# A two-layer encoder trunk on one Trainium2 core: the first layer's output projection as seven quarter products, and all five queues in an order read from a table

## The chip, the core and the metric

The kernel runs on one core of one Trainium2 chip. The metric is the device time of one execution in microseconds (us). Three executions of the kernel before took 652.29, 652.94 and 653.63 us; their median is 652.94 us. The engines are named as the profile names them: PE (TensorE, matmuls), PEld (its weight loads), DVE (VectorE), ACT (ScalarE), POOL (GpSimd), SP (SyncE, which issues most loads and stores).

## The reference

512 tokens of width 1024 pass two layers. Layer 0 mixes tokens with neighbourhood attention on a grid 64 wide (16 heads of 64), layer 1 with multi-head latent attention (MLA, 16 heads, dense over the 512 tokens). Both have the same frame:

```python
for i in range(2):
    xn = rmsnorm(x, norm_g[i])
    y = mixer_na(xn, ...) if i == 0 else mixer_mla(xn, ...)   # (heads(xn) * silu(z)) @ w_out
    h = x + y
    gate = sigmoid(rmsnorm(h, ple_norm[i]) @ ple_w_gate[i])
    x = h + gate * (p[i] @ ple_w_proj[i])
return rmsnorm(x, final_norm)
```

The mixer's input projection also gives `z`, as wide as the heads' outputs together. `w_out` and `ple_w_gate[i]` are 1024x1024. The change bears on `(heads * silu(z)) @ w_out` of layer 0 and on the order in which everything is issued.

## The kernel before

**Products.** Every float32 product is made of three matmuls on halves: an operand is copied to a rounded `hi` (ACT), `lo` is the rest (a subtraction on POOL or DVE), and hi·hi, lo·hi and hi·lo are added up in one PSUM bank. A weight piece (128x1024, 512 KB) is loaded by SP into one of three buffers `wraw`, ACT makes `hi` of it, POOL makes `lo` (`load_w`, L89 to L106; ACT's line is L100, the subtraction L101). A full 1024x1024 product over 512 tokens is 8 banks of 24 matmuls of 128x512, 192 in all (`out_proj`, L622 to L636).

**Seven products.** The values of layer 0 (`values_seven`) and the two gate matrices (`gate_seven`, L775) are already computed by a scheme of Strassen's kind: both operands are cut into quarters, seven products of sums of quarters replace eight, and 168 matmuls do the work of 192. The weight sums are made ahead in device memory by DMAs that POOL issues, some of them accumulating (`sum_step`, L726 to L730, eight of 1 MB for a matrix). The sums for layer 0's gate are made in heads 0 to 7 of layer 0, those for layer 1's gate in heads 8 to 15 (`na_heads`: `l, step = divmod(j, 4)`, where `j` is a pair of heads).

**Heads of layer 0.** For a pair `j`, `attend` (L493) calls `na_head` twice. One head makes scores on PE (L558, L559, bank `ps_S`), takes maxima on DVE (L565), exponentials on ACT (L576), reciprocals on DVE (L578), the normalization on POOL (L582, four instructions a head), transposes on PE (L594, L596, bank `ps_T`), splits the turned weights into `ph` and `pl`, and multiplies with the values (L608, bank `ps_O`). `combine` adds the two halves (L220 on ACT, L221 on DVE) and `gated` (L223 to L229) multiplies by `z` on POOL and splits into `oh` and `ol`. The last three `z` (NLATE) come after the last pair.

**The seam.** After the heads, `out_proj` does its 192 matmuls. Each bank is added to the residual `r` by DVE (L635), eight additions of 128x512, and handed to `turn_h` (L1258), which scales it, transposes it and lets `keep_half` (L745) form the operands of `gate_seven` from it.

**MLA heads.** In layer 1 `mla_heads` (L942) walks 64 quarter heads: scores (L123, `ps_S`), maximum on DVE (L1052), exponential on ACT (L1054), reciprocal on DVE (L1055), normalization on POOL (L1056), four transposes (L155), and products with the values (L1071). Projections of later heads (L959) fill PE in between. Queries are partly moved by DMA (`qe<-rl`).

**Order.** The program is traced as Python runs, and a scheduler that simulates a timeline then orders each engine's instructions (`schedule_with_timeline_sim`, in `kernel`). Some forty places pin an instruction behind another with `tc.issue_after`, among them the class `InOrder` (L41) and the chains of matmuls in `out_proj` and `gate_seven`. What a queue holds runs strictly in that queue's order.

## Time and profile before

| | |
|---|---|
| runs shown | 652.29, 652.94, 653.63 us; median 652.94 |
| the profiled execution | 653.56 us; span 651.5 us, granted clock 0.995 |
| outside the span | 653.56 - 651.5 = 2.06 us |
| busy share of the span | PE 98%, PEld 83%, ACT 70%, DVE 66%, POOL 63% |
| moved by DMA | 107.41 MB, mean 165 GB/s |

The span runs from the first to the last instruction of the profiled execution, which is itself one of the runs. A busy time counts the records of an engine as a union in time; a matmul's record includes its way through the array, so that the distance between the starts of neighbouring matmuls (their pitch) is what one of them costs in a row. In a timeline a row groups like instructions that follow each other: start, length, engine, line, operation, output and inputs, count, and in brackets the idle time before it and what ended that. Windows give each engine's busy time in a stretch with its count, then the granted PE clock, the DMA share and the GB/s. POOL's records overlap: the next one starts before the last has ended, and here too the pitch is the cost.

### The profile page before, as it was taken

What the parts mean: (1) busy time and instruction counts of PE and PEld (TensorE: products, weight loads), DVE (VectorE), ACT (ScalarE), POOL (GpSimd) and SP (SyncE); (2) the same over time, 40 slices, a digit from 0 to 9 for tenths busy, and PEclk for the clock granted to TensorE, in tenths of its full rate; (3) what the DMA queues carried; (4) which work ended last, traced back from release to release, by engine and by line L of the source; (5) the groups of instructions that cost most, each with busy time, mean ns of one, the idle gap of its engine ahead of it and who ended that gap; (6) DMA issues with size and microseconds to landing.
All of it is one profiled execution on the core that took longest, in us unless ns stands there. A gap on an engine that the chain in (4) does not pass through costs nothing.

```text
span 651.5 us, 9980 instructions
## 1 busy us (share of the span) xinstructions
PE 640.2 (98%) x3299; PEld 541.9 (83%) x3299; DVE 427.7 (66%) x886; ACT 453.4 (70%) x903; POOL 408.4 (63%) x371
## 2 busy tenths in 40 slices
PE   9999999999999999999999999999999999999994
PEld 6888878888888888888999887888888888888884
DVE  6197987565665616569715514898988885474665
ACT  7575766887886733788644535897989897547855
POOL 0471006877978853797655516786969887437974
PEclk9999999999999999999999999999999999999997
DMA  9939725778958989446643245120112223683524
GB/s 326 355 124 306 217 66 179 263 205 217 229 209 217 239 178 342 147 154 188 224 140 102 78 109 156 32 75 24 49 50 66 65 84 112 229 292 126 193 65 162
DMA packets 46131, 107.41 MB, mean 165 GB/s; under 512 B 4736, under 2 KB 17792, under 8 KB 46080
## 3 DMA queue, kind: packets, MB, share of 16 engines
q1 hardware_dynamic: 34608, 87.12, 39.3%
q0 software_dynamic: 11040, 18.88, 13.6%
q10 hardware_dynamic: 432, 0.79, 0.3%
q8 instruction: 26, 0.43, 0.3%
q14 instruction: 25, 0.20, 0.1%
HBM read 95.23 MB, written 25.17 MB: 185 GB/s over the span
## 4 chain that ended last, share of the span: by engine, by line
PE 83%; POOL 1%; ACT 1%; DVE 0%; DMA 0%; issue 0%; POOLq 0%
PE ps_mm L123 27%; PE ps_S L123 10%; PE ps_mm L959 7%; PE ps_T L155 6%; PE ps_T L851 5%; PE ps_O L1071 5%; PE ps_mm L851 3%; PE ps_S L851 3%; PE ps_O L608 2%; PE ps_T L123 2%; PE ps_O L123 2%; PE ps_mm L909 2%; PE ps_T L301 2%; PE ps_T L596 2%; PE ps_S L909 1%; PE ps_S L559 1%
## 5 line engine op out<-in xcount | busy, mean ns | idle before, releaser
L101 POOL TENSOR_TENSOR wwlo<-wraw,wwhi 128x1024 fp32r<-128x1024 f32 (+5 forms) x68 | 122.3, 1810 | 93.5 <-ACT wwhi L100 41.9
L796 POOL TENSOR_TENSOR wlo<-wraw,whi 128x512 fp32r<-128x512 f32 x56 | 72.7, 1331 | 22.3 <-ACT whi L794 20.2
L1056 POOL TENSOR_TENSOR ex<-ex,rc 128x512 f32<-128x512 f32 x64 | 66.2, 1043 | 26.6 <-DVE rc L1055 22.5
L100 ACT ACTIVATE wwhi<-wraw 128x1024 fp32r<-128x1024 f32 (+5 forms) x71 | 55.1, 799 | 34.3 <-PE ps_mm L123 18.9
L1054 ACT ACTIVATE ex<-ps_S,mx 128x512 f32<-128x512 f32 x64 | 44.0, 687 | 12.6 <-DVE mx L1052 10.9
L1052 DVE TENSOR_REDUCE mx<-ps_S 128x1 f32<-128x512 f32 x64 | 43.7, 683 | 8.4 <-PE ps_S L123 7.7
L582 POOL TENSOR_TENSOR ex<-ex,rc 128x128 f32<-128x128 f32 (+1 forms) x64 | 37.5, 701 | 17.7 <-DVE rc L578 17.5
L112 DVE TENSOR_TENSOR pt_lo<-ps_T,pt_hi 128x512 fp32r<-128x512 f32 x64 | 43.1, 680 | 7.1 <-ACT pt_hi L110 6.7
L110 ACT ACTIVATE pt_hi<-ps_T 128x512 fp32r<-128x512 f32 x64 | 37.7, 594 | 3.4 <-PE ps_T L155 3.0
L155 PE MATMUL ps_T<-ident,ex 128*128 128x128 f32 x256 | 38.3, 272 | 0.0
L155 PEld LDWEIGHTS ps_T<-ident,ex 128*128 128x128 f32 x256 | 31.5, 140 | 7.5
L123 PE MATMUL ps_mm<-xh,wwhi 128*128 128x512 f32 x120 | 33.7, 404 | 0.0
L221 DVE TENSOR_TENSOR u<-ps_O,u 64x512 f32<-64x512 f32 x32 | 21.9, 685 | 17.7 <-ACT u L220 17.2
L576 ACT ACTIVATE ex<-ex,mx 128x128 f32<-128x128 f32 (+1 forms) x64 | 30.2, 473 | 4.2 <-DVE mx L565 4.1
L123 PE MATMUL ps_mm<-xl,wwhi 128*128 128x512 f32 x120 | 31.9, 395 | 0.0
L794 ACT ACTIVATE whi<-wraw 128x1024 fp32r<-128x1024 f32 x28 | 29.3, 1057 | 3.2 <-DMA wraw<-sum 2.4
L123 PE MATMUL ps_mm<-xh,wwlo 128*128 128x512 f32 x120 | 31.1, 394 | 0.0
L123 PE MATMUL ps_S<-ke,qe 96*128 96x512 f32 x96 | 28.9, 407 | 0.3 <-DMA qe<-rl 0.3
L123 PE MATMUL ps_S<-ko,qo 128*128 128x512 f32 x96 | 28.9, 409 | 0.0
L959 PE MATMUL ps_mm<-cT,wwhi 128*128 128x512 f32 x94 | 27.7, 393 | 0.0
L220 ACT ACTIVATE u<-ps_O 64x512 f32<-64x512 f32 x32 | 18.9, 591 | 12.0 <-PE ps_O L608 8.8
L225 POOL TENSOR_TENSOR u<-u,z 128x512 f32<-128x512 f32 x16 | 22.6, 1412 | 7.5 <-DVE u L221 7.5
(488 smaller groups left out, 1915.1 us busy)
## 6 DMA issues: line engine op xcount, KB each, us to landing
sum<-gate POOLq DMA_DIRECT2D x12, 1024.0 KB, 8.2
wraw<-na_qk SPq DMA_DIRECT2D x16, 512.0 KB, 4.9
wraw<-sum SPq DMA_DIRECT2D x16, 512.0 KB, 3.3
pe<-pe SPq DMA_DIRECT2D x31, 256.0 KB, 5.9
wraw<-gate SPq DMA_DIRECT2D x12, 512.0 KB, 3.3
wraw<-na_v SPq DMA_DIRECT2D x10, 512.0 KB, 3.4
sum<-sum POOLq DMA_DIRECT2D x4, 1024.0 KB, 11.1
wraw<-na_o SPq DMA_DIRECT2D x8, 512.0 KB, 4.8
```

What stands on the lines that cost most here:

```text
L100: nc.scalar.activation(hi[:, c], raw[:, c], AF.Copy)
L101: f = lambda e, c=c: e.tensor_tensor(out=lo[:, c], in0=raw[:, c], in1=hi[:, c].bitcast(F32), op=ALU.subtract)
L110: self.last_copy = self.act.activation(hi, src, AF.Copy, scale=scale)
L112: self.dve.tensor_tensor(out=lo, in0=src, in1=hi.bitcast(F32), op=ALU.subtract)
L123: last = self.last_mm = nc.tensor.matmul(out, l, r, start=i == 0, stop=i == n - 1)
L155: self.last_mm = self.nc.tensor.transpose(t[:, i * P:(i + 1) * P], b, self.ident)
L796: nc.gpsimd.tensor_tensor(out=lo[:, o], in0=raw[:, o], in1=hi[:, o].bitcast(F32), op=ALU.subtract)
L851: mm = nc.tensor.matmul(ps, l, r, start=j == 0 and p in banks, stop=j == 11 and p in (2, 3, 4), skip_group_check=True)
L959: self.last_mm = nc.tensor.matmul(PS[key], *terms[i], start=i == 0, stop=i == len(terms) - 1)
L1052: nc.vector.reduce_max(mx, sp, axis=AX.X, negate=True)
L1054: nc.scalar.activation(ex, sp, AF.Exp, bias=mx, accum_out=sm)
L1056: nc.gpsimd.tensor_tensor(out=ex, in0=ex, in1=rc.to_broadcast([P, S]), op=ALU.mult)
```

## The change

1. **Seven products for layer 0's output projection** (`MIXED = (0,)`, `out_seven`): 7 products x 2 token halves x 12 = 168 matmuls of 128x512 take the place of 192. Its weights come in 14 pieces instead of 8 (6 from `na_o`, 8 from sums); the products' banks are 1, 7 and 6, and the four others are added on in the same banks. The left operands need sums as well: `gated_seven` forms them per `oT` block in halves of 256 columns, `mixes` takes three differences of 128x256 on DVE for four blocks, `cast` splits them. The additions into the residual become 18 instead of 8 (`adds`), all on DVE, and `keep_mixed` keeps the residual's halves in mixed form. The gate of layer 0 takes its products in the order 1, 7, 6, 2, 5, 3, 4.
2. **Sums in other places**: the eight DMAs for `na_o` are issued in heads 0 to 7 of layer 0, those for layer 0's gate in heads 8 to 15, and those for layer 1's gate in MLA heads 1 to 8.
3. **Heads in parts**: `na_head` ends after the normalization; the transposes with their splits (`na_turn`) and the products with the values (`na_out`) are functions of their own. In the last pair both heads' scores come first, then the late `z`, then a string `BEFORE` gives the order of what is left; a string `INSIDE` gives that of `out_seven`.
4. **The order**: all `issue_after` pins go. `ORDER` holds a permutation of each engine's traced instructions, and `in_order` ties every instruction behind the one before it in that list. The scheduler has nothing left to choose on the five queues, in the whole program.

The diff, cut to its core (the table is one line of some 190):

```diff
+MIXED = (0,)
+BEFORE = """t00 t01 m0 W70w W71w g5 g6 h0 t10 t11 W20w h1 g7"""
+INSIDE = """
+W21vd P10 P11 m01 y01 a10 m02 y02 a11 W40vd P70 P71 W41v a70 m03 y03 a71 W60vd W61vd
...
-            with self.tc.issue_after(self.last.ins) if self.last is not None else nullcontext():
-                self.last = call(*args, **kw)
+            self.last = call(*args, **kw)
...
             for j in range(8):
-                l, step = divmod(j, 4)
-                if step == 0:
-                    self.quarters(l)
-                attend(j, lambda e: self.sum_step(l, 2 * step + e))
-            late = range(8 - NLATE, 8)
-            zs.update(self.z_phase(a["na_z"], xT, late, self.last_exp.ins))
-            for j in late:
-                self.gated(U[j], zs[j], oT, j)
+                key = (("out", 0), ("gate", 0))[j // 4]
+                if j == 5:
+                    self.W, self.oT = {}, oT
+                    for c in range(2):
+                        self.out_piece(None, 0, 1, c, str(c))
+                (attend if j < 7 else lambda j, also: last_pair(also))(j, lambda e: self.sum_step(key, 2 * (j % 4) + e))
...
+    def gated_seven(self, u, zs, oT, j):
+        z = zs[j]
+        self.pool.tensor_tensor(out=z, in0=u, in1=z, op=ALU.mult)
+        g, k = divmod(j, 4)
+        hi, lo = (oT[s][g][:, k, :] for s in range(2))
+        if g == 0:
+            self.pool.tensor_tensor(out=u[:, HI], in0=z[:, LO], in1=z[:, HI], op=ALU.subtract)
+            for x, c in ((z, LO), (u, HI)):
+                self.act.activation(hi[:, c], x[:, c], AF.Copy)
+                self.pool.tensor_tensor(out=lo[:, c], in0=x[:, c], in1=hi[:, c].bitcast(F32), op=ALU.subtract)
+            return
+        self.act.activation(hi, z, AF.Copy)
+        (self.pool if j == 4 else self.dve).tensor_tensor(out=lo, in0=z, in1=hi.bitcast(F32), op=ALU.subtract)
...
+        def product(p, i, mm):
+            m = [(x[s][:, k, o + i * P:o + (i + 1) * P], W[p][k // 2][r][:, k % 2 * S:(k % 2 + 1) * S])
+                 for c in range(2) for s, r in ((0, 0), (1, 0), (0, 1)) for k in (2 * c, 2 * c + 1)]
+            for j, (l, r) in enumerate(m):
+                self.last_out = nc.tensor.matmul(ps, l, r, start=j == 0 and p in banks,
+                                                 stop=j == 11 and p in (2, 4, 3), skip_group_check=True)
...
             nc.vector.reciprocal(rc, sm)
-            nc.gpsimd.tensor_tensor(out=ex, in0=ex, in1=rc.to_broadcast([P, S]), op=ALU.mult)
+            norm = nc.gpsimd.tensor_tensor(out=ex, in0=ex, in1=rc.to_broadcast([P, S]), op=ALU.mult)
+            step = h - 1
+            if qt == 1 and 0 <= step < 8:
+                self.sum_step(("gate", 1), step)
...
+ORDER = dict(
+    PE=(
+        "0-10 23 29-30 24-25 31-32 11-12 26 13 35 14-16 20-21 27 53 17-19 41 47 42-43 48-50 54 51 36 28 22 37-38 52 63 "
...
+def in_order(tc):
+    behind = mybir.DependencyInfo(mybir.DependencyClass.NoSync, mybir.DependencyReason.DATA)
+    for e, runs in ORDER.items():
+        mine = [i for i in traced if i.engine == getattr(mybir.EngineType, engines[e])]
...
+        for x, y in zip(order, order[1:]):
+            tc.add_manual_dep(y, x.name, behind, reason="in_order")
```

Three places show what the order does. First PE at the start of the output projection. Before, the first two banks (`ps_S_2697`, `ps_S_2737`) take their matmuls in runs of two, from the weight pieces `wwhi_2599` and `wwhi_2605` and the operands `oh0`, `ol0`:

```order
L596 MATMUL ps_T_2388<-ident_71,ex_2351 128x128 x4
L123 MATMUL ps_S_2697<-wwhi_2599,oh0_1000 128x512 x2
L123 MATMUL ps_S_2697<-wwhi_2599,ol0_1002 128x512 x2
L123 MATMUL ps_S_2697<-wwlo_2600,oh0_1000 128x512 x2
L123 MATMUL ps_S_2697<-wwhi_2605,oh0_1000 128x512 x2
L123 MATMUL ps_S_2697<-wwhi_2605,ol0_1002 128x512 x2
```

Now products 1 (`ps_T_2666`, `ps_T_2679`, from the early pieces `w0` and `w1`) and 7 (`ps_mm_2715`, `ps_mm_2728`, from `whi_2565`) run mixed with each other, behind the last head's product with the values and the last late `z`:

```order
L643 MATMUL ps_O_2619<-pl_2609,Q11_510 128x256
L138 MATMUL ps_S_2516<-xh1_166,wwlo_2512 128x512 x3
L837 MATMUL ps_T_2666<-w0_2047,oh0_1007 128x512
L837 MATMUL ps_T_2679<-w0_2047,oh0_1007 128x512 x2
L837 MATMUL ps_T_2666<-w0_2047,oh0_1007 128x512
L837 MATMUL ps_T_2679<-w0_2047,ol0_1009 128x512
L837 MATMUL ps_mm_2715<-whi_2565,oh0_1007 128x512
L837 MATMUL ps_mm_2728<-whi_2565,oh0_1007 128x512
```

The matmuls of two products alternate one by one where a bank took its own in pairs before.

Second POOL in heads 10 and 11 of layer 0. Before, a head's four normalizations (`ex`) stand together, then one sum's DMA and one weight piece's `lo` (`wwlo`, 128x1024):

```order
L101 TENSOR_TENSOR wwlo_2472<-wraw_2470,wwhi_2471 128x1024
L582 TENSOR_TENSOR ex_2029<-ex_2029,rc_2032 128x128
L582 TENSOR_TENSOR ex_2029<-ex_2029,rc_2032 128x256 x3
L730 DMA sum17_105<-gate 1024x256
L101 TENSOR_TENSOR wwlo_2505<-wraw_2503,wwhi_2504 128x1024
L582 TENSOR_TENSOR ex_2087<-ex_2087,rc_2090 128x128
L582 TENSOR_TENSOR ex_2087<-ex_2087,rc_2090 128x256 x3
L730 DMA sum14_102<-gate 1024x256
```

Now the same heads (`ex_2060`, `ex_2118`), with the early pieces `w0` and `w1` and a half of `ol0` among them:

```order
L757 DMA sumgate05_99<-gate 1024x256
L774 TENSOR_TENSOR w0_2047<-wraw_2046,w0_2047 128x512 x2
L774 TENSOR_TENSOR w1_2053<-wraw_2052,w1_2053 128x512
L614 TENSOR_TENSOR ex_2060<-ex_2060,rc_2063 128x256
L614 TENSOR_TENSOR ex_2060<-ex_2060,rc_2063 128x128
L116 TENSOR_TENSOR wwlo_2218<-wraw_2216,wwhi_2217 128x1024
L614 TENSOR_TENSOR ex_2060<-ex_2060,rc_2063 128x256
L774 TENSOR_TENSOR w1_2053<-wraw_2052,w1_2053 128x512
L757 DMA sumgate04_98<-gate 1024x256
L614 TENSOR_TENSOR ex_2060<-ex_2060,rc_2063 128x256
L614 TENSOR_TENSOR ex_2118<-ex_2118,rc_2121 128x128
L614 TENSOR_TENSOR ex_2118<-ex_2118,rc_2121 128x256
```

More stands between a head's normalizations than before, and they are interrupted by work for the output projection.

Third PE in a MLA head. Before, quarter head `ps_S_5274` is followed by these rows, and its own transposes (of `ex_5279`) come only behind three more quarter heads (`ps_S_5300`, `ps_S_5336`, `ps_S_5363`) and the transposes of three others:

```order
L123 MATMUL ps_S_5274<-ke00_3473,qe00_3469 128x512
L123 MATMUL ps_S_5274<-ke01_3474,qe00_3469 128x512
L123 MATMUL ps_S_5274<-ke00_3473,qe01_3470 128x512
L959 MATMUL ps_mm_5283<-cT0_3467,wwhi_4942 128x512 x2
L959 MATMUL ps_mm_5283<-cT1_3468,wwhi_4942 128x512 x2
L155 MATMUL ps_T_5290<-ident_71,ex_5201 128x128 x4
L123 MATMUL ps_S_5300<-ko00_3475,qo00_3471 128x512
```

Now, for the same quarter head (`ps_S_5361`, then `ex_5366`):

```order
L138 MATMUL ps_S_5361<-ke00_3552,qe01_3549 128x512
L138 MATMUL ps_S_5387<-ko00_3554,qo00_3550 128x512
L138 MATMUL ps_S_5387<-ko01_3555,qo00_3550 128x512
L138 MATMUL ps_S_5387<-ko00_3554,qo01_3551 128x512
L170 MATMUL ps_T_5377<-ident_71,ex_5287 128x128 x4
L1102 MATMUL ps_mm_5370<-cT1_3547,wwhi_5026 128x512
L1102 MATMUL ps_mm_5370<-cT0_3546,wwlo_5027 128x512 x2
L170 MATMUL ps_T_5411<-ident_71,ex_5310 128x128 x3
L1214 MATMUL ps_O_5418<-pt_hi_5270,vt_4767 128x512 x2
L1214 MATMUL ps_O_5418<-pt_hi_5270,vt_4799 128x512
L138 MATMUL ps_S_5423<-ko00_3554,qo00_3550 128x512
L138 MATMUL ps_S_5423<-ko01_3555,qo00_3550 128x512
```

One more matmul of `ps_S_5423` and two transposes follow, then the transposes of `ex_5366`: twelve matmuls of 128x512 and nine transposes stand between.

393 lines of the change are left out of this document (259 added, 134 removed), and 177 rows, old and new, of tables (ACT, DVE, PE, POOL).

## The prediction

> **What bounds the kernel now.** The first view is the page: span, busy shares, granted clock.
>
> ```profile
> span 651.5 us, 9980 instructions
> ...
> PE 640.2 (98%) x3299; PEld 541.9 (83%) x3299; DVE 427.7 (66%) x886; ACT 453.4 (70%) x903; POOL 408.4 (63%) x371
> ...
> PEclk9999999999999999999999999999999999999997
> ```
>
> PE is busy nearly from end to end at full clock. But a busy PE counts overlapping records, so 98% alone does not say that taking matmuls away shortens the run. Two further views do: PE's waits over the whole run (line, what it waited for, total, times, longest), and a timeline of PE in the output projection.
>
> ```profile
> PE ps_T L301 <- ACT s L51: 1.2, 1, 1.2
> PE ps_T L1187 <- PEq L1464: 0.8, 1, 0.8
> PE ps_T L596 <- POOL ex L582: 0.3, 1, 0.3
> PE ps_S L123 <- DMA qe<-rl: 0.3, 1, 0.3
> ```
>
> ```profile
> 251.94 1.07 PE L123 MATMUL ps_mm<-ww,oh 128*128 128x512 f32 x4
> 252.85 1.07 PE L123 MATMUL ps_S<-ww,oh 128*128 128x512 f32 x4
> ...
> 260.11 1.47 PE L155 MATMUL ps_T<-ident,hg 128*128 128x128 f32 x12
> 261.34 0.71 PE L123 MATMUL ps_O<-ww,oh 128*128 128x512 f32 x2
> ```
>
> PE waits four times, 2.6 us in 651.5. In between it moves at a fixed pitch: (252.85 - 251.94) / 4 = 0.2275 us, call it 0.227, for a 128x512 matmul, (261.34 - 260.11) / 12 = 0.103 us for a transpose. So PE's stream sets the time, and what the change does is the sum of what it takes out of this stream and of the waits that it makes or ends. The profiled execution took 653.56 us, 0.62 above the median of the runs shown (652.94); the sum is made against 653.56, and 0.62 comes off at the end. About 0.2%, 1.3 us, is what a measurement here can tell from no change.
>
> **The products.** 168 matmuls replace 192: 24 x 0.227 = 5.45 us less on PE. They stand in a stretch where PE is full, so the whole of it counts if nothing else comes to decide there. Nothing else on PE changes in number; the table cuts the runs of transposes into 133 pieces instead of 128 by the order, which I take at 0.03 us a break, an estimate between nothing and the 0.06 that half the difference of the two pitches would be: 0.15.
>
> **The engines beside PE in the seam.** Windows of 10 us (PE, PEld, DVE, ACT, POOL busy with counts; clock, DMA share, GB/s) show what is free.
>
> ```profile
> 220.00:230.00 10.00, 9.67 (x58) 8.23 (x57) 5.24 (x18) 7.27 (x17) 7.79 (x11) 1.00 1.07 244
> 230.00:240.00 10.00, 10.00 (x50) 8.41 (x49) 1.86 (x3) 3.87 (x6) 5.87 (x4) 1.00 0.72 120
> 240.00:250.00 10.00, 10.00 (x50) 8.42 (x49) 4.26 (x3) 4.07 (x5) 5.32 (x3) 1.00 0.92 342
> 250.00:260.00 10.00, 10.00 (x46) 8.28 (x45) 6.43 (x9) 2.12 (x2) 2.41 (x1) 1.00 0.87 327
> ...
> 260.00:300.00 40.00, 40.00 (x194) 33.41 (x193) 26.73 (x39) 33.17 (x53) 33.11 (x28) 1.00 0.49 163
> ```
>
> DVE gets ten more additions of 128x512 into the residual, twelve differences of 128x256 from `mixes`, and the subtractions for six more weight pieces and the new operands. At the rows below this is 10 x 0.69 = 6.9 us, 12 x 0.42 = 5.0 us, and for the 21 halves of 128x512 more in its count 21 x 0.68 = 14.3 us: 26 us.
>
> ```profile
> L814 DVE TENSOR_TENSOR r<-r,ps_T x4: 675/686/686, 305.7 to 639.0; 128x512 f32<-128x512 f32 x4
> L814 DVE TENSOR_TENSOR r<-r,ps_O x1: 412/412/412, 644.0 to 644.0; 128x256 f32<-128x256 f32 x1
> ```
>
> From 220 to 260 DVE has 40 - 17.8 = 22 us free, and from 260 to 300 13 more, so 26 fit into 35. ACT has 22 us free in the same 40 and gets six copies of 128x1024 (6.4 us by the row of L794 below) and twelve of 128x256. I cost both at nothing; if the cover were gone, each would hand PE the last addition or cast before a product, 0.7 us at a time.
>
> **POOL in the heads.** This is the engine whose room shrinks most. Its rows in heads 8 to 10, with the pitch read from one start to the next:
>
> ```profile
> 161.79 2.90 POOL L101 TENSOR_TENSOR wwlo<-wraw,wwhi 128x1024 fp32r<-128x1024 f32 x1
> 164.15 1.47 POOL L582 TENSOR_TENSOR ex<-ex,rc 128x128 f32<-128x128 f32 x2
> 165.22 1.63 POOL L225 TENSOR_TENSOR u<-u,z 128x512 f32<-128x512 f32 x1
> 166.47 1.51 POOL L582 TENSOR_TENSOR ex<-ex,rc 128x256 f32<-128x256 f32 x2
> ...
> 173.88 2.12 POOL L582 TENSOR_TENSOR ex<-ex,rc 128x128 f32<-128x128 f32 x4 [0.94 <-DVE rc L578]
> 175.93 0.80 POOL L730 DMA_DIRECT2D sum<-gate  x1
> 176.74 0.98 POOL L582 TENSOR_TENSOR ex<-ex,rc 128x128 f32<-128x128 f32 x2
> ```
>
> So a head's normalizations cost 2.05 us, a `lo` of 128x1024 2.36, a 128x512 step 1.25, a DMA issue 0.81; a 128x256 half I put at 0.64. From head 8's first normalization to head 12's last the changed order holds on POOL 5 x 2.05 + 4 x 2.36 + 7 x 1.25 + 4 x 0.81 + 8 x 0.64, and 0.8 of small ones: 37.6 us. PE's own rows from the end of head 8's scores to head 12's transposes come to 42.1 us at the pitches. From a head's scores to its first normalization the chain of maximum, exponential and reciprocal takes about 2.5 us, which leaves some 39.6 us: POOL has 2 us to spare. Before, head 8 to 15 had 39.1 us of POOL in 56.8 of PE; now it is 51.7 in 58.3. I take no stall, with an upper bound of 3 us.
>
> In return the tightest places of the heads get wider. Before, counted from the order at PE's pitches, one head's transposes come 2.7 us after its scores (head 9) and another's 3.6 (head 14), where the median is 7.2; there PE waits for `ex L582`, and the timeline shows the gap to be wider than the 0.3 of the waits.
>
> ```profile
> 220.79 0.33 PE L608 MATMUL ps_O<-ph,Q 128*128 128x192 f32 x1
> 221.45 0.33 PE L596 MATMUL ps_T<-ident,ex 128*128 128x128 f32 x1 [0.33 <-POOL ex L582]
> ```
>
> From 220.79 to 221.45 stands one matmul of 0.11: 0.55 us lost. By the order the shortest such distance is now 5.8 us, the median 10.0. I take -0.55.
>
> **The weights of the seam.** 14 pieces replace 8, so 28 pieces feed 336 matmuls (76.3 us) where 22 fed 360 (81.7 us).
>
> ```profile
> wraw<-sum SPq DMA_DIRECT2D x16, 512.0 KB, 3.3
> ...
> wraw<-gate SPq DMA_DIRECT2D x12, 512.0 KB, 3.3
> ...
> wraw<-na_o SPq DMA_DIRECT2D x8, 512.0 KB, 4.8
> ```
>
> ```profile
> L796 POOL TENSOR_TENSOR wlo<-wraw,whi 128x512 fp32r<-128x512 f32 x56 | 72.7, 1331 | 22.3 <-ACT whi L794 20.2
> ...
> L794 ACT ACTIVATE whi<-wraw 128x1024 fp32r<-128x1024 f32 x28 | 29.3, 1057 | 3.2 <-DMA wraw<-sum 2.4
> ```
>
> A piece holds one of three buffers for 3.3 to 4.8 us of landing, 1.06 of ACT and 2.66 of POOL, so three buffers give a piece every (3.3 + 1.06 + 2.66) / 3 = 2.3 us, at 4.8 every 2.8 us. Five pieces are there before the seam begins, 23 are left: 53 to 65 us, under 76.3. Single pieces are tight: from the earliest possible issue to the first use PE has 7.5 us of work for one gate piece, 8.6 and 9.6 for two others, where before it had 15 to 35 in this stretch; 4.4 to 5.9 are needed. I take nothing here; below nothing isn't possible, since no wait for these loads stands in PE's list now.
>
> **The MLA heads.** Eight DMA issues of 0.81 us come to POOL among the normalizations. More weighs that the table brings transposes nearer to their scores. One chain, read from the timeline:
>
> ```profile
> 439.72 0.40 PE L123 MATMUL ps_S<-ke,qe 96*128 96x512 f32 x1
> ...
> 440.16 0.69 DVE L1052 TENSOR_REDUCE mx<-ps_S 128x1 f32<-128x512 f32 x1 [0.17 <-PE ps_S L123]
> ...
> 440.88 0.69 ACT L1054 ACTIVATE ex<-ps_S,mx 128x512 f32<-128x512 f32 x1 [1.09 <-DVE mx L1052]
> ...
> 441.69 0.16 DVE L1055 RECIPROCAL rc<-sm 128x1 f32<-128x1 f32 x1 [0.84 <-ACT ex L1054]
> ...
> 442.00 1.04 POOL L1056 TENSOR_TENSOR ex<-ex,rc 128x512 f32<-128x512 f32 x1 [0.83 <-PE ps_O L1071]
> ```
>
> Scores end at 440.12, the normalized weights at 443.04: 2.9 us if no queue is in the way. Before, the shortest distance on PE was 6.2 us; now it is 3.7 at one place (12 x 0.227 + 9 x 0.109) and 4.4 to 5.4 at six more, so 0.8 us of room at the worst. One other instruction in front of it on DVE or ACT takes 0.6 to 0.7, one on POOL 1.04. The waits on PE are now 0.3 here. The bounds are 0 and about seven places x 0.5 = 3.5 us; I take 1.2, nearer to nothing, because at six of the seven the room is over 1.4 us.
>
> **Start and tail.** After PE's last matmul 8.7 us of scaling, statistics and stores remain; the last bank's halves are now mixed, so that the first half is ready 0.9 us later. DVE came to the first half late anyway, at 642.84, when PE was done with both halves: 0 to 0.5, I take 0.2.
>
> ```profile
> 642.39 0.40 PE L851 MATMUL ps_O<-wlo,X 128*128 128x256 f32 x2
> ...
> 642.84 0.42 DVE L811 TENSOR_TENSOR ps_S<-pe,ps_S 128x256 f32<-128x256 f32 x1
> ```
>
> **Sum.** -5.45 + 0.15 - 0.55 + 1.2 + 0.2 = -4.45: 653.56 - 4.45 = 649.1, less 0.62 is 648.5 us.
>
> **The rivals.** *The table also ends the other waits.* If the waits of 1.2, 0.8 and 0.3 us go as well and no new one comes, it is -5.45 + 0.15 - 0.55 - 2.3 + 0.2 = -7.95, 645.0 us. For it speaks that all of them are waits that an order can move; against it that the 0.8 is PE's own sequencer at the very start, and that the distances in MLA became shorter. Chance 0.14.
>
> *POOL becomes the bound.* With 37.6 of 39.6 us used, it takes a lengthening by 5% for POOL to decide over head 8 to 12. The trace has a reason:
>
> ```profile
> L225 POOL TENSOR_TENSOR u<-u,z x16: 1282/1298/1819, 134.0 to 562.7; 128x512 f32<-128x512 f32 x16
> ```
>
> The same step takes 1.28 us at best and 1.82 at worst. If DVE's work beside it, which grows, lengthens POOL's by 15%, 37.6 become 43.2, 3.6 us more than there are; with the MLA waits at their upper half, 2 us, the gain is nearly gone: -5.45 + 0.15 - 0.55 + 3.6 + 2 + 0.2 = -0.05, 652.9 us. The median of 1.298 speaks against it, few steps being lengthened. The Trainium skill, GPSIMD Engine Reference, section Specifications, speaks for this rival: GpSimd's SBUF interfaces are shared with VectorE, and they contend with DVE instructions that read two SBUF inputs, as `mixes` and the `lo` subtractions moved to DVE do; by it alone the lengthening would be expected, and the row's spread agrees with it. Chance 0.12.
>
> *The seam waits for its weights (slower).* If landing under load takes longer, the three buffers pace the seam. The point is 76.3 / 23 = 3.32 us a piece, that is a landing of 6.2 us, against 3.3 to 4.8 now. At 7.5 us it is 23 x (7.5 + 3.72) / 3 = 86.0 us, 9.7 more than PE needs: 653.56 - 4.45 + 9.7 - 0.62 = 658.2 us. For it: the DMA share is already 0.87 to 1.07 there, the weights grow by 3 MB, and every queue is now in one fixed order, in which a late piece holds back all behind it on ACT and POOL. Against it: sums, the larger part of the new pieces, land in 3.3 us. The Trainium skill, TensorE: Matmul & The Clock Gate, section on the HAM clock gate, adds that TensorE's clock falls to half after some 3.4 us of idling; the longest wait in this trace is 1.2 us, so no run here shows it, and by it a stall of that length would cost more than itself. Chance 0.16.
>
> That the change doesn't do what it says can be left aside, since the matmuls are counted from the order.
>
> **How the numbers follow.** Forecast 0.58, the rivals 0.14, 0.12 and 0.16. The first two are faster by over 0.2% (below 651.6), 0.72, and a little of the POOL case, 0.02; the rest of that case is within 0.2%, 0.10; the slower case 0.16. The likeliest case's own range is 647.0 to 651.6: below, no new wait and no tail (-1.4); above, 3.1 of the 5.6 that the bounds of MLA, POOL and tail add together. The range reaches to 644.0 below and to 655.5 above, which takes in the first two rivals and the lower part of the third.
>
> **What would show it.** Right: a 128x512 pitch still at 0.227, 168 matmuls at the projection, PE's waits under 4 us in all, none at `L596`'s successor in heads 9 and 14, POOL below 95% in heads 8 to 12. Wrong: a PE wait of over 1 us for `wraw` pieces, `whi` or `wlo` between 220 and 300, PE waits for POOL's `ex` in the heads, or many waits of half a microsecond in MLA.

## The result, and the profile after

The changed kernel takes 656.89 us (median of 6 executions, 655.06 to 659.58); the kernel before took 653.03 beside it (6 executions, 652.29 to 653.63). The ratio is 1.0062, 95% interval 1.0040 to 1.0084: slower by 3.9 us, where 4.4 us faster was forecast. The profiled execution took 657.0 us. Its page:

```profile
span 655.2 us, 9979 instructions
...
PE 638.7 (97%) x3275; PEld 537.2 (82%) x3275; DVE 442.1 (67%) x931; ACT 465.3 (71%) x921; POOL 421.9 (64%) x392
...
PEclk9999999999999899999999999999999999999998
```

PE has its 24 matmuls less (3299 to 3275), and one slice of the clock's row, the fourteenth, shows an 8 where before had nines. PE's waits:

```profile
PE ps_O L643 <- DVE u L235: 2.3, 1, 2.3
PE ps_S L138 <- ACT whi L685: 1.4, 1, 1.4
PE ps_T L170 <- DVE cn L159: 1.3, 1, 1.3
PE ps_T L837 <- DVE r L61: 1.1, 1, 1.1
PE ps_T L1329 <- PEq L1828: 0.8, 1, 0.8
```

They come to 6.9 us in place of 2.6. None is for POOL's `ex`, none for a weight piece in the seam; three of the four long ones are for VectorE, the fourth (1.4) stands at the very start, at 4.39 us. The pitch is the old one, (269.71 - 268.81) / 4 = 0.225 us, from PE's timeline:

```profile
268.81 1.07 PE L997 MATMUL ps_mm<-whi,X 128*128 128x512 f32 x4
269.71 0.39 PE L997 MATMUL ps_mm<-wlo,X 128*128 128x512 f32 x1
```

So the products gave what they should. To see where more than that was lost, the distance from each PE start to the next, less the pitch of the first one's shape, is added up by stretches of the span. This is worked out from the two traces and is no view of the profile:

```
us of PE above its pitch     before   after    difference
  0 to  80                     0.42     0.86      +0.44
 80 to 100                     1.48     0.07      -1.41
100 to 220 (heads)             0.59     1.62      +1.03
220 to 260 (seam)              0.66     6.04      +5.38
260 to 340                     0.41     1.22      +0.81
340 to 400                     0.24     1.98      +1.74
400 to 560 (MLA heads)         2.92     2.79      -0.13
560 to the last matmul         0.12     0.47      +0.35
```

The differences make +8.2; with the products' -5.45, PE's last matmul ends 2.8 us later (645.6 in place of 642.8). Behind it stand 9.6 us instead of 8.7. 2.8 + 0.9 is the 3.7 by which the span grew. Two thirds of the loss lie in the seam. Its windows, as in the prediction (busy of PE, PEld, DVE, ACT, POOL; clock, DMA share, GB/s):

```profile
220.00:230.00 10.00, 7.70 (x38) 6.33 (x37) 6.58 (x16) 7.06 (x14) 6.38 (x8) 0.83 0.74 115
...
240.00:250.00 10.00, 8.85 (x39) 6.71 (x37) 9.97 (x18) 2.81 (x5) 2.74 (x2) 1.00 0.68 241
250.00:260.00 10.00, 10.00 (x46) 8.13 (x47) 9.96 (x17) 4.34 (x6) 0.00 (x0) 1.00 0.58 199
```

DVE is full from 240 to 260 (it had 4.26 and 6.43 there before), and POOL does nothing from 250 to 260. The first gap, one piece of the timeline each of POOL, DVE and PE:

```profile
216.69 1.66 POOL L757 DMA_DIRECT2D sumgate<-gate  x1
217.51 2.17 POOL L61 TENSOR_TENSOR wlo<-wraw,whi 128x512 fp32r<-128x512 f32 x1
218.76 2.15 POOL L800 TENSOR_TENSOR ol<-z,oh 128x512 fp32r<-128x512 f32 x1
...
217.81 3.39 DVE L61 TENSOR_TENSOR z<-z 128x256 f32<-128x256 f32 x1
...
224.55 0.67 DVE L235 TENSOR_TENSOR u<-ps_O,u 64x512 f32<-64x512 f32 x1
...
222.67 0.40 PE L138 MATMUL ps_S<-xl,wwhi 128*128 128x512 f32 x1
225.37 0.33 PE L643 MATMUL ps_O<-ph,Q 128*128 128x192 f32 x1 [2.30 <-DVE u L235]
```

One `mixes` step, `z<-z`, takes 3.39 us where ten of the eleven others take 0.40 to 0.42 (one takes 1.04). It begins 0.3 us after the first of POOL's two steps beside it and ends 0.3 us after the second has ended. Everything that DVE has behind it, the maxima and reciprocals of the next head and at last the addition into `u`, comes 3 us later, and PE stands still for 2.5 us. Behind the gap the granted clock falls:

```profile
225.00:227.00 2.00, 1.63 (x8) 1.56 (x9) 0.99 (x3) 1.68 (x4) 1.58 (x2) 0.66 0.41 65
227.00:229.00 2.00, 2.00 (x9) 1.70 (x9) 1.12 (x3) 1.22 (x2) 1.43 (x2) 0.50 0.03 4
```

PE's excess between 220 and 240 is 4.23 us, the gap's 2.47 and some 1.6 of slow matmuls. The same picture stands at the first MLA norms, where the table puts two DMA issues and a weight part on POOL beside two tiny steps of DVE:

```profile
364.89 1.68 POOL L757 DMA_DIRECT2D sumgate<-gate  x2
366.56 2.40 POOL L116 TENSOR_TENSOR wwlo<-wraw,wwhi 128x1024 fp32r<-128x1024 f32 x1
...
365.79 3.30 DVE L1071 TENSOR_TENSOR cn<-tp 128x16 f32<-128x16 f32 x2
369.01 0.47 DVE L159 SCALAR_TENSOR_TENSOR cn<-c,rs,gkv 128x256 f32<-128x256 f32 x1
```

### The profile page after: what moved, and what is told of

Its sections match the earlier page's. It is cut to its first block, busy times and chain, and to the rows that moved or that the text cites. A ratio compares the mean times of both kernels' runs of the same rounds, so it can differ in the third digit from the quotient of the medians.

```text
span 655.2 us, 9979 instructions
## 1 busy us (share of the span) xinstructions
PE 638.7 (97%) x3275; PEld 537.2 (82%) x3275; DVE 442.1 (67%) x931; ACT 465.3 (71%) x921; POOL 421.9 (64%) x392
## 4 chain that ended last, share of the span: by engine, by line
PE 91%; DVE 3%; POOL 2%; ACT 1%; issue 1%; DMA 1%; POOLq 0%; DVEq 0%; ACTq 0%
PE ps_mm L138 23%; PE ps_S L138 11%; PE ps_mm L1102 7%; PE ps_T L170 6%; PE ps_O L1214 5%; PE ps_T L997 4%; PE ps_mm L997 3%; PE ps_mm L425 3%; PE ps_T L314 3%; PE ps_S L837 3%; PE ps_S L997 2%; PE ps_O L643 2%; PE ps_mm L1052 2%; PE ps_T L138 2%; PE ps_mm L214 2%; PE ps_S L314 2%
## 5 line engine op out<-in xcount | busy, mean ns | idle before, releaser
L116 POOL TENSOR_TENSOR wwlo<-wraw,wwhi 128x1024 fp32r<-128x1024 f32 (+5 forms) x66 | 115.0, 1758 | 58.4 <-PE ps_O L314 26.3
L774 POOL TENSOR_TENSOR wlo<-wraw,whi 128x512 fp32r<-128x512 f32 x42 | 55.6, 1355 | 16.4 <-ACT whi L772 16.0
L115 ACT ACTIVATE wwhi<-wraw 128x1024 fp32r<-128x1024 f32 (+5 forms) x68 | 52.3, 788 | 18.4 <-DMA wraw<-mla_z 4.7
L614 POOL TENSOR_TENSOR ex<-ex,rc 128x256 f32<-128x256 f32 (+1 forms) x64 | 38.0, 707 | 16.3 <-DVE rc L610 15.7
L61 POOL TENSOR_TENSOR wlo<-wraw,whi 128x512 fp32r<-128x512 f32 x16 | 22.6, 1427 | 27.8 <-ACT whi L61 26.2
L138 PE MATMUL ps_mm<-xh,wwlo 128*128 128x512 f32 x112 | 33.8, 403 | 0.0
L61 ACT ACTIVATE whi<-wraw 128x1024 fp32r<-128x1024 f32 x22 | 23.0, 1052 | 11.5 <-DMA wraw<-na_v 3.8
L1102 PE MATMUL ps_mm<-cT,wwhi 128*128 128x512 f32 x94 | 29.2, 403 | 0.0
L601 DVE CUSTOM_DVE_ANT_0 ex<-ps_S,bias 128x256 f32<-128x256 f32 x48 | 19.2, 419 | 9.5 <-PE ps_T L631 6.0
```

The source lines that it names most:

```text
L61: self.last = call(*args, **kw)
L115: nc.scalar.activation(hi[:, c], raw[:, c], AF.Copy)
L116: f = lambda e, c=c: e.tensor_tensor(out=lo[:, c], in0=raw[:, c], in1=hi[:, c].bitcast(F32), op=ALU.subtract)
L138: last = self.last_mm = nc.tensor.matmul(out, l, r, start=i == 0, stop=i == n - 1)
L774: (rest or self.pool).tensor_tensor(out=lo[:, o], in0=raw[:, o], in1=hi[:, o].bitcast(F32), op=ALU.subtract)
L1102: self.last_mm = nc.tensor.matmul(PS[key], *terms[i], start=i == 0, stop=i == len(terms) - 1)
```

## The experiments

**The theory.** A VectorE step with both inputs in SBUF does not begin to work while a GpSimd step with two inputs runs; the change puts such steps side by side at places where PE hangs on DVE's next steps. Rivals: a DMA issue on POOL holds DVE; or DVE's added work alone fills the seam, and the long steps only show where.

**m1_lock and m2_lock: the hold by itself.** Two probes hold nothing but six DVE steps of 128x256, between a start and an end that both engines share, with different company on POOL. Each ran once.

> A probe that computes nothing of the reference (its output is left-over tiles): seven short phases in which DVE and POOL start together, six DVE subtractions of 128x256 beside six POOL steps of 128x512 or four DMA issues. Theory (DVE's step with two SBUF inputs cannot run beside a POOL step and waits for it to end): alone the six DVE steps take 6 x 0.35 us; beside POOL products of two SBUF inputs they take as long as POOL's steps, 1.3 us and more each; with one input in PSUM they stay at 0.35 to 0.42. Rival (the long step in the changed kernel waited for something else, a semaphore or its data): beside POOL the DVE steps keep 0.35 to 0.5 us in every phase. The phases with DMA issues tell whether those hold DVE back as well; no theory is sure of that.

```profile
8.67 2.72 DVE L29 TENSOR_TENSOR y<-x,v 128x256 f32<-128x256 f32 x6
...
21.03 7.43 DVE L29 TENSOR_TENSOR y<-x,v 128x256 f32<-128x256 f32 x6
...
30.30 2.69 DVE L29 TENSOR_TENSOR y<-x,ps 128x256 f32<-128x256 f32 x6
...
39.16 3.30 DVE L29 TENSOR_TENSOR y<-x,v 128x256 f32<-128x256 f32 x6
...
49.63 2.73 DVE L29 TENSOR_TENSOR y<-x,v 128x256 f32<-128x256 f32 x6
```

From the top: alone; beside POOL steps with two inputs; beside the same with one DVE input in PSUM; beside POOL steps with one input; beside POOL's DMA issues. Only the second is held, 7.43 us for six: the first step begins before POOL's and takes 0.42, the other five take 1.37 each, as long as one POOL step. Beside POOL's steps with one input two of the six take 0.71, the rest 0.42. A DMA issue alone holds nothing, though only two of the six steps stand beside one (0.43 each). POOL itself pays less, 8.40 us for its six steps in place of 7.96. The first rival is out for an issue by itself, but the step of 3.39 us is longer than any POOL step beside it. Hence the second probe, whose last phase puts one issue and then three steps on POOL.

> The probe again (its output is left-over tiles), now with POOL's steps written to two tiles in turn, so that none waits for the one before it: alone; beside six DVE subtractions of two SBUF inputs; 128x256 POOL steps beside them; DVE steps with SBUF and PSUM inputs in turn; one DMA issue and then three POOL steps. Theory (back-to-back POOL steps leave DVE no gap, so that one DVE step waits through two or three of them, as the 3.4 us step in the changed kernel did): single DVE steps of 2.5 us and more. Rival (DVE gets its turn after each POOL step): 1.2 us for each DVE step, and the 3.4 us must have another reason.

POOL's six steps alone, the same steps beside DVE's six, and then that last phase:

```profile
9.62 7.36 POOL L54 TENSOR_TENSOR w<-p,q 128x512 f32<-128x512 f32 x6
...
17.74 8.40 POOL L54 TENSOR_TENSOR w<-p,q 128x512 f32<-128x512 f32 x6
...
17.59 7.43 DVE L30 TENSOR_TENSOR y<-x,v 128x256 f32<-128x256 f32 x6
...
42.66 0.97 POOL L50 DMA_DIRECT2D sums<-gate  x1
43.66 3.71 POOL L54 TENSOR_TENSOR w<-p,q 128x512 f32<-128x512 f32 x3
...
42.66 6.84 DVE L30 TENSOR_TENSOR y<-x,v 128x256 f32<-128x256 f32 x6
```

Without an issue ahead the rival came true: DVE gets its turn after every POOL step, five times 1.37 us, although POOL's steps stand ready behind one another; and here POOL's own six grow by 14%, 7.36 to 8.40 us. In the last phase the theory came true: of the 6.84 us one step takes 4.54, from 43.12 until 0.3 us behind POOL's third step; the others take 0.42. So behind a DMA issue a step can be held through a whole run of POOL steps. Both long steps of the changed kernel begin during a DMA issue too. That an issue is needed is not shown: in e1 below a mix takes 3.17 us beside two POOL steps with no issue just ahead of them.

**How the next kernels are made.** Each is the changed kernel with single entries of the table moved. In `in_order`, for each engine:

```diff
+        for what, behind_it in MOVES.get(e, ()):
+            moved = [mine[n] for n in what]
+            order = [i for i in order if i not in moved]
+            k = order.index(mine[behind_it]) + 1
+            order[k:k] = moved
```

`([292, 293], 274)` under DVE puts DVE's traced steps 292 and 293 right behind its step 274. Nothing else differs.

**e1_mix_late: the first two mixes later.**

```diff
+MOVES = {"DVE": [([292, 293], 274)]}
```

> The changed kernel with the first two differences of mixes for block 0 moved on DVE, behind the sum u of head 14 (L235) that PE waits for. Theory (that difference, 3.39 us instead of 0.42, holds up the maxima and the sum behind it, and the 2.5 us of idle PE then cost another 1.6 us at a lower clock): PE's wait of 2.3 us goes and the time falls by 3 to 4 us, to 653 to 654. Rival (the heads' end is too tight in this order whatever stands there): a wait of 1.5 us or more stays at the same place, 656 or more.

655.93 us, ratio 1.0046 (1.0031 to 1.0061). The hold moved along: two mixes now take 4.09 us together from 222.40 (0.88 and 3.17), and PE waits 1.8 us there, for `pl` (the low half of the turned weights). It is the rival's number, by the theory's mechanism.

**e2_pool_late: POOL's two steps later.**

```diff
+MOVES = {"POOL": [([131, 89], 124)]}
```

> The changed kernel with DVE's order as it is, but two POOL steps (a lo half of the weight piece for product 7 and the lo of oT block 4) moved behind head 15's normalizations. Theory (POOL's two steps hold DVE's difference): the difference takes 0.4 to 1.3 us instead of 3.39 though DVE's own order is the same, and the time falls by 3 to 4 us to 653 to 654. Rival (the difference is long by itself or by DVE's queue): it stays at 3 us, 656 or more.

654.72 us, ratio 1.0024 (1.0012 to 1.0035), 2.2 us less than the change as it was. The same mix, not touched itself, in DVE's timeline:

```profile
218.26 0.42 DVE L61 TENSOR_TENSOR z<-z 128x256 f32<-128x256 f32 x1
```

The gap at 222.67 and the lower clock are gone. The wait for `r` at L837 grew to 1.8 us, and a new one of 0.7 stands at L643. Worked out as in the table, PE's excess fell from 4.23 to 1.09 us between 220 and 240 and grew from 1.81 to 2.35 between 240 and 260. The hold is shown as the cause of the first gap, and part of the gain is given back at the next place; the time stays above the theory's 653 to 654.

**e3_sched: the seven products without the table.** The call of `in_order` is left out, so that the scheduler orders the queues.

```diff
-        in_order(tc)
```

> The changed kernel without the forced order: the table stays unused, the scheduler orders the five queues, the seven products stay. Theory (the table's tight places cost about 8 us, the products save 5.45): 648 to 650. Rival (the products' own extra work on DVE and POOL makes the seam wait in any order): 653 or more, with waits for DVE or POOL between 215 and 260.

769.62 us, ratio 1.176. Theory and rival both missed: the change took out the old pins with the old order, so this is no "products alone". It says nothing on the table against the kernel before. Nor does any run hold the old projection under a table, so what the table costs or gains by itself stays open.

**e4_adds: e2, and two additions of `r` earlier.**

```diff
+MOVES = {"POOL": [([131, 89], 124)], "DVE": [([317, 318], 316)]}
```

> The kernel with POOL's two steps moved (as in the run before), and on DVE the two additions of product 1's second half moved ahead of a weight half and a difference of mixes that have two SBUF inputs. Theory (these two, lengthened beside POOL to 1.4 and 1.5 us, are why PE waits 1.8 us for r at 245): that wait goes, the time falls by 1.5 to 2 us from 654.7 to 652.7 to 653.2. Rival (DVE is full in the seam, another wait takes its place): 654 or more, a new wait for DVE between 240 and 262.

653.31 us, ratio 1.0004 (0.9995 to 1.0014). It is 0.1 us above the theory's range and below the rival's. Four moved instructions took back 3.6 of the 3.9 us. PE's gaps over 0.6 us are now 0.83 at 228.96, 0.70 at 245.97, 1.46 at 364.73, and the start's.

**e5_cn and e6_tail** went for the norm at 365 and for the tail.

```diff
+ e5: as e4, and "DVE": ([480, 481], 473)
+ e6: as e5, and "DVE": ([842], 837), ([834], 844); "PE": the last 12 matmuls of ps_S ahead of those of ps_O
```

> As the kernel with the moved additions, and the two rotary differences of 128x16 (cn from tp) of the third token block moved on DVE ahead, into a gap before POOL's DMA issues and weight piece. Theory (they wait 3.2 us for POOL there, and hold the normalization that PE waits for): the wait of 1.3 us for cn goes and 1.4 us with it, to 651.3 to 651.8. Rival (the scaling behind them reads two SBUF inputs as well and now waits in their place): no change, a DVE step of 2 us or more at the same place.

> As the kernel before it, and the tail: PE does the last 12 matmuls of the first half of the last bank ahead of those of the second half, and DVE takes the second half's product ahead of the first half's addition, with one scaling of another row moved behind the statistics. Theory (the tail of the changed kernel is 0.9 us longer because a 0.75 us scaling stands ahead of the last addition and the halves end together): 0.7 to 1.0 us less, 650.4 to 651. Rival (the stores set the end): within 0.3 us of the kernel before it.

e5: 653.59 us. One of the two steps moved was the wrong one, so a `cn<-tp` of 3.24 us stayed, and the wait with it: inconclusive. e6: 654.07 us; the last scaling of DVE begins 4.55 us behind PE's end (e4: 4.44), so these moves don't shorten the tail. What lengthened it stays open.

**e7_clear and e8_dma: e4's three gaps at once.** e7 moves three mixes behind the addition that PE waits for, one addition earlier, and both `cn<-tp` ahead of POOL's issues; e8 takes the norm from POOL's side instead.

```diff
+ both: "POOL": ([131, 89], 124); "DVE": ([317, 318, 326], 316), ([294, 305, 306], 300)
+ e7: "DVE": ([480, 478], 473)
+ e8: "POOL": ([228, 252], 206)
```

> The second e4 with the three gaps that it has left on TensorE taken one by one, in VectorE's order alone: the three mixes that stood as 2.97 us ahead of the add u<-ps_O that TensorE waited for go behind it, the add r<-r,ps_mm that TensorE waited for goes ahead of a weight part and a mix, and both cn<-tp steps of the sixth norm go ahead of GpSimd's two DMA issues (e5 had moved one of them and another step). Theory (each gap is a VectorE step that stands late in its queue, because of steps held beside GpSimd, and the place is not full otherwise): the gaps of 0.83, 0.70 and 1.46 us shrink below 0.3 us each, together 2.4 to 2.9 us less than e4's 653.3: 650.4 us to 651.0. Rival (VectorE has no room in these places, whatever is put first makes the next one late): the gaps come back within 5 us of the same places, 652.5 us to 653.5. Further expected by the theory: cn<-tp takes 0.14 to 0.17 us in the sixth norm, and z<-z still takes over 0.8 us where it stands beside GpSimd, with nobody waiting.

> As e7, but the sixth norm's gap is taken from GpSimd's side: VectorE's order there stays that of the change, and GpSimd's two DMA issues go behind its 128x1024 weight part wwlo and two further steps. Theory (a VectorE step with both inputs in SBUF is held until the GpSimd step with two inputs beside it ends, and a DMA issue ahead of it only lengthens the stretch): wwlo starts right after GpSimd's power step, at about 361.7 us of e4's clock, and ends 2.4 us later, so cn<-tp, due 0.85 us after its start, takes 1.4 to 1.7 us for both instead of 3.3, the norm's second half is ready 0.4 us or more before TensorE asks, its gap is below 0.3 us, and the time is e7's within 0.4 us. Rival (the DMA issues themselves hold VectorE): cn<-tp takes under 0.3 us, since no issue stands beside it; the time is the same.

656.62 us (1.0037 to 1.0065) and 654.88 us (1.0022 to 1.0043): the theory missed by 6 and 4 us, for three reasons that the traces show. In e7's norm the two steps were quick, and the hold fell on the next one with two SBUF inputs:

```profile
365.44 0.22 DVE L1071 TENSOR_TENSOR cn<-tp 128x16 f32<-128x16 f32 x2
...
366.92 3.48 DVE L159 SCALAR_TENSOR_TENSOR cn<-c,rs,gkv 128x256 f32<-128x256 f32 x1
```

In e8, with the issues behind the weight part, the hold fell on the step ahead of the two and lasted 2.45 us, where the two had taken 3.30; they then stood beside nothing but DMA issues:

```profile
363.73 2.45 DVE L159 SCALAR_TENSOR_TENSOR cn<-c,rs,gq 128x384 f32<-128x384 f32 x1
366.10 0.25 DVE L1071 TENSOR_TENSOR cn<-tp 128x16 f32<-128x16 f32 x2
366.27 0.47 DVE L159 SCALAR_TENSOR_TENSOR cn<-c,rs,gkv 128x256 f32<-128x256 f32 x1
```

That gap is gone, 1.65 us to 0.50 in the stretch from 360 to 380. The gap near 229 was never DVE's; in e8 DVE stood idle there for a copy of ACT:

```profile
228.95 0.68 DVE L61 TENSOR_TENSOR u<-ps_O,u 64x512 f32<-64x512 f32 x1 [1.01 <-ACT u L61]
```

And the three mixes had readers: ACT's `oh` came later, DVE's long queue behind it too, and two new gaps of 1.72 and 1.45 us came (at 242.14 and 248.50 in e8).

**e9_dma_add and e10_u.** e9 is e4 with e8's cure of the norm and the earlier addition of e7 and e8, without their moved mixes; e10 adds ACT's copy ahead of a weight part.

```diff
+ both: "POOL": ([131, 89], 124), ([228, 252], 206); "DVE": ([317, 318, 326], 316)
+ e10: "ACT": ([286], 287); "DVE": ([306], 297)
```

> e4 with two of its three remaining gaps taken and the mixes back at e4's place, since e7 and e8 showed that ScalarE's oh and through it VectorE's later steps hang on them: GpSimd's two DMA issues behind wwlo as in e8, and the add r<-r,ps_mm ahead of a weight part and a mix. Theory (what costs is the place of a few steps, and each gap has its own chain, which is cleared or not): the gap near 365 goes from 1.46 us to about 0.3 (e8 had 0.50 in the whole stretch of 20 us against 1.65), the gap near 246 from 0.70 to under 0.1 because the add comes 1.1 us earlier (0.67 and 0.41 us of steps that stood ahead of it), the gap of 0.83 near 229 stays: 651.2 us to 651.8, which is below the kernel before. Rival (the seam is full, the gap near 246 returns as a wait of ScalarE or VectorE at the next accumulation): 652.0 to 653.3.

> e9, and the gap of 0.83 us near 229 taken from its real end: e8 showed there that VectorE stood idle for 1.01 us, waiting for ScalarE's copy u<-ps_O, which stands behind a weight part whi of 1.05 us. ScalarE's copy goes ahead of that part, and VectorE's third mix goes behind the add that reads the copy. Theory: the copy ends at about 228.1 us of e4's clock instead of 229.2, the add 0.7 us later or behind two mixes, at about 229.0, when TensorE asks at 229.2; the gap is below 0.2 us and the time 0.6 to 0.8 us below e9's: 650.4 us to 651.2. Rival (GpSimd's weight part that waits for whi and the mix behind come late for others): the same as e9 within 0.3 us or slower.

653.18 us (0.9993 to 1.0011) and 654.61 us (1.0012 to 1.0031): the rival both times. In e9 both gaps went as foreseen, and one of 1.93 us came at 247.13. There PE waits for a weight part of ACT that stands behind `Yh`, and `Yh` waits for the last mix (`Yh` and `Yl` are the two halves of the mixed left operand); in e10 PE waited 0.2 us instead of 0.7 for `u`, and then 1.1 for `pl`, which stands behind the moved mix. At this point the second rival, that the seam is full whatever the order, was ahead.

**e12_one_input and e13_narrow: holds against work.** e12 keeps order and work and takes the holds away; e13 keeps order and holds and takes work from the mixes.

```diff
+ e12: if op == ALU.subtract: return g.tensor_scalar(out, in1, 2.0 ** -12, None, op0=ALU.mult)
+ e13: w = slice(c.start, c.start + 1), and v likewise, in place of the 256 columns of each mix
```

> The changed kernel in its own order, with every subtraction on GpSimd replaced by a scaling of its second input alone (hi times 2 to the power -12), so that GpSimd's weight parts and low parts have one input; the low halves are then not those of the reference. GpSimd's products with two inputs stay. Theory (what makes the changed kernel slower is VectorE's steps held beside GpSimd's steps with two inputs): z<-z near 218 takes under 1.1 us instead of 3.39, cn<-tp near 366 under 0.8 instead of 3.30, the gaps at 222.67 (2.47, and the lower clock behind it) and 367.98 (1.46) shrink below 0.5: 651.0 us to 652.5. It can lose a part of that, since the probe's one-input step took 1.53 us beside VectorE where the one with two took 1.29. Rival (VectorE's work in the seam is simply too much, the hold only shows where): gaps of the same sum, 655 us to 657.

> The changed kernel in its own order, with each of the twelve mixes done on 128x1 instead of 128x256, so that VectorE keeps the instruction and its place, and 0.25 us or more of its work goes each time; the mixed values are then wrong. Theory (held steps): a step with both inputs in SBUF is held whatever its size, so the first mix near 218 still takes 3 us or more, the gaps at 222.67 and 367.98 stay, and only the gap of 1.27 at 248.40, where VectorE's queue is unbroken, shrinks: 654.5 us to 656.5. Rival (work): 3 to 4 us of VectorE's time in the seam are freed, the gaps at 222.67 and 248.40 go: 651.0 us to 653.0.

e13: 654.85 us (1.0015 to 1.0044), inside the theory's range and 1.9 us above the rival's upper end. It is also 2.0 us below the changed kernel, at the edge of what the two intervals can tell, so the work of the mixes may count for a part of the loss. The first mix has one column and is held as before, and the clock falls behind the gap of 2.21 us as before (timeline, then window):

```profile
217.72 3.13 DVE L61 TENSOR_TENSOR z<-z 128x1 f32<-128x1 f32 x1
```

```profile
225.00:227.00 2.00, 1.99 (x9) 1.91 (x10) 1.12 (x2) 1.34 (x3) 1.49 (x3) 0.56 0.32 50
```

Among the gaps the one at 248 shrank most, 1.27 to 0.76, as DVE's unbroken queue got shorter. e12: the holds are gone. All DVE steps that take over 0.6 us more than the median of their form (operation and shape) lose 16.0 us together in the changed kernel, 1.9 in e12 (and 23.4 in the kernel before). The twelve mixes take 559 ns on average, and the gaps at 222 and 368 do not stand. But the time is 670.86 us, outside both expectations. DVE's group, then PE's waits:

```profile
L61 DVE TENSOR_TENSOR z<-z 128x256 f32<-128x256 f32 x12 | 6.6, 559 | 0.1
```

```profile
PE ps_T L631 <- POOL ex L1750: 2.9, 3, 1.9
PE ps_T L170 <- POOL ex L1750: 2.9, 5, 0.9
PE ps_T L629 <- POOL ex L1750: 2.5, 2, 2.2
```

POOL's step with one input is the slower one (1522 ns mean for the 58 weight halves of 128x512, where the same 58 with two inputs took 1375 in the changed kernel), and POOL becomes late in the heads. So e12 confirms the mechanism of the long steps and can't price them.

**e11_yh, e15_yl, e14_yl_u: single steps into DVE's idle time.** In e9 DVE stood idle for 2.94 us before the unbroken queue, waiting for ACT's `oh`. e11 puts the four mixes for `Yh` there. e15 adds an earlier `Yl`, e14 in addition e10's cure with the mix further back.

```diff
+ e11: as e9, "DVE": ([312, 313, 322, 323], 300)
+ e15: as e11, "DVE": ([325], 315)
+ e14: as e15, "ACT": ([286], 287); "DVE": ([306], 295)
```

> e9, and of the four mixes that feed ScalarE's Yh (128x256 each) all go ahead of the step ol<-z,oh at which VectorE stood idle for 2.94 us in e9, waiting for ScalarE's oh. In e9 the last of them stood at 246.68 us and ended 0.04 us before Yh began, and TensorE waited 1.8 us for the product of Yh. Theory (in the seam VectorE runs one unbroken queue from 235.6 to 252 us of e9's clock, so a step late in it is as late as all that is put ahead of it; what counts is which step stands in the idle 2.94 us): the four are done by about 235.4, Yh no longer waits for VectorE, the gap of 1.93 near 247 goes and with it the lower clock behind it: 650.5 us to 651.5. Rival (the queue has no room, the wait comes back at the next step, as in e7 to e10): 652.5 to 653.5.

> e11, and the low part Yl that TensorE waited 0.63 us for near 259 moved ahead of three weight parts, two steps of r and hg and a mix, to a place where its inputs have been there for some us. Theory: the gap of 0.79 near 258 goes below 0.3 us and nothing else in the seam comes late, so the time is 0.4 to 0.8 us below e11's 652.96: 652.2 us to 652.6; single executions spread from about 650.5 to 654, since in e7, e11 and e12 loads that landed 2 to 4 us later than in other executions left gaps of 1 to 2 us between 60 and 100. Rival (queue full): 652.7 to 653.5.

> e15, and the gap of 0.84 us near 229 taken from ScalarE's side as in e10 (the copy u<-ps_O ahead of the weight part), but with VectorE's third mix behind the two low parts pl as well, since in e10 TensorE waited 1.1 us for pl behind that mix. Theory (a gap has its own chain and goes when the whole chain is cleared): that gap below 0.3 us, the time 0.4 to 0.8 us below e15's. Rival (the mix held later makes VectorE's queue later for the rest of the seam): e15's time within 0.3 us or slower, with a new wait between 230 and 260.

e11: 652.96 us (0.9994 to 1.0011), the rival's number; its fastest execution took 651.21. The gap at 247 did not come back; 1.29 us stand above the pitch from 240 to 260 in place of e9's 3.83. The median moved little, and the profiled execution, the slowest at 654.55, shows why in part: from 60 to 100 it lost 2.2 us that e9's did not, 1.03 of them in one gap at a wait for ACT's `s`. e15: 652.90 us (0.9985 to 1.0009) beside 653.1 for the kernel before: the same time, and the rival's number again, though the gap near 258 went. Its profiled execution took 652.22, and PE's waits come to 2.1 us, where before had 2.6:

```profile
PE ps_T L1329 <- PEq L1836: 0.8, 1, 0.8
PE ps_O L643 <- DVE u L61: 0.7, 1, 0.7
PE ps_S L138 <- ACT whi L685: 0.4, 1, 0.4
PE ps_mm L997 <- ACT whi L61: 0.2, 1, 0.2
```

e14: 653.87 us (0.9997 to 1.0015), the rival; it took 0.5 us from the gap near 229 and brought one of 1.02 at 242.87. No version tried beats the kernel before by more than a measurement can tell.

So the seam's large gaps can be cleared when each step is followed to its readers. But the loss did not all go: from 220 to 270 PE's excess is 0.8 us before, 6.2 after, 2.6 in e4 and 2.7 in e15, where the 1.05 us won from 240 to 260 against e4 came back as 1.09 from 260 to 270, in small pieces. What e15 gained on e4 lies at the MLA norms (1.87 to 0.68 from 340 to 400). DVE is as full in e15 as it was in the changed kernel:

```profile
230.00:240.00 10.00, 10.00 (x48) 8.43 (x49) 9.44 (x12) 6.29 (x10) 6.88 (x5) 1.00 0.83 298
240.00:250.00 10.00, 9.99 (x45) 7.98 (x44) 9.99 (x18) 3.16 (x4) 2.73 (x2) 1.00 0.60 213
250.00:260.00 10.00, 10.00 (x48) 8.11 (x47) 9.37 (x16) 5.77 (x7) 0.00 (x0) 1.00 0.66 218
```

So the second rival keeps a part: of the 5.4 us that the seam lost, 3.6 went with the places of a few steps, and at least 1.8 stayed in every order tried. POOL (the fifth busy time) stands idle from 250 to 260 beside a full DVE; no run gave it some of DVE's `lo` steps, so whether another division of the work would clear the rest was not tested.

Nor do these orders bring the forecast: e15's PE ends 2.0 us before that of the kernel before (640.8 to 642.8) instead of 5.45, since 3.5 us more lie above the pitch, in one gap of 0.84 at 228.79 and many places of 0.1 to 0.5 us; and its tail is the longer one, 9.6 us to 8.7.

## Why the prediction was wrong, point by point

- **The products, -5.45:** right, in count and pitch.
- **The stall at 220.79, -0.55:** right; no PE wait for POOL's `ex` is left in the heads.
- **The pieces, +0.15:** too small. From 100 to 220, with no PE wait of over 0.3 us in either kernel, the distances above the pitch grew by 1.0 us, and e15 has 3.5 us of them on the whole span. Which of the cut runs and short distances they come from was not separated.
- **DVE in the seam, "26 fit into 35. I cost both at nothing":** this is the step that failed. The count of work was fair (17.8 us busy from 220 to 260 became 32.5), but a sum of free time doesn't say that the steps find it when they are due: the queue is in a fixed order, some steps take 3.4 us instead of 0.42, and from 240 to 260 no free time is left. The seam lost 5.4 us where nothing was put down. "0.7 us at a time" was also the wrong price for a lost cover: the gaps were 2.47, with 1.6 of lower clock behind it, and 1.27.
- **POOL in the heads, no stall:** right, with the margin as thin as worked out: e12 lengthens POOL's weight parts by 11% and stalls PE there.
- **The seam's weights, nothing:** right; the slower rival that was named, of buffers and landings, did not happen.
- **MLA, +1.2:** did not come. 2.92 us above the pitch became 2.79; 0.8 us of room at the tightest place was enough.
- **Left out:** the gap of 1.46 at the MLA norms. The two DMA issues were seen among POOL's steps, but not what stands beside them on DVE. On the other side the wait of 1.2 at L301 went (-1.4 from 80 to 100), which only the first rival had; in part that is luck of the profiled execution, since gaps of 1.08 and 1.03 us stand there again in those of e5 and e11.
- **Tail, +0.2:** it was 0.9.

"POOL becomes the bound" named the right resource and turned it round. It let DVE's work lengthen POOL's steps by 15%. In the probes POOL's grew by 6% and, where no step waits for the one before it, by 14%, so the size was fair; but DVE's grew by 173% (2.72 to 7.43), and the waits on PE were for DVE. The outliers that it read on POOL (1.28 to 1.82) were the small side of the matter; DVE's own outliers stood in the trace of before too, 23.4 us of them, off PE's path. Beside these rows stands the Trainium skill, SBUF — State Buffer, section Summary: rules for kernel authors: if DVE has two SBUF inputs while the GpSimd operation reads SBUF, the second one to issue blocks fully until the first has finished. The first three probe rows agree with it; the fourth, 3.30 us beside POOL steps with one input, shows no full block. The prediction's sentence on the Trainium skill speaks of contention, and not of a block.

The range, 644.0 to 655.5, missed by 1.4 us. It was short because DVE in the seam was put at nothing and added nothing to the upper bound.

## What to carry over

Before work is given to an engine with free time, look at what stands beside each step on the engine that can hold it (here POOL, by the probes), and whether the engine that sets the time hangs on the next steps in that queue: here steps of 0.15 to 0.42 us cost 3 us. Look for such long steps in the trace of before, off the critical path too, since a new order can bring them onto it. And when a gap is cleared by moving a step, follow all its readers: in seven of the ten reordered kernels above that aimed at the seam, a wait came back somewhere else.
